# Hybrid decoder layer on one core: ScalarE evacuates the early up-projections, VectorE adds the carried columns

## The chip, the cores and the metric

The kernel runs on one core of one Trainium2 chip. The metric is the device time of one execution in microseconds (us). Engines are named as in the profile: PE is TensorE (PEld its weight loads), DVE is VectorE, ACT is ScalarE, POOL is GpSimd, SP is SyncE, whose queue issues all DMA transfers here.

## The reference

One layer of a hybrid decoder on 1024 tokens of width 1024, in float32. A mixer (RWKV-7 heads beside a causal convolution of width 31) is followed by a gated feed-forward network whose hidden channels pass a causal depthwise convolution of width 3. Cut to what matters here:

```python
D_MODEL, SEQ, D_FF, FFN_CONV_WIDTH = 1024, 1024, 2816, 3

def _conv_ffn(h, ffn_up, ffn_conv_w, ffn_conv_b, ffn_down):
    hid = h @ ffn_up.astype(h.dtype)                       # (1, 1024, 5632)
    hid = _causal_dwconv(hid, ffn_conv_w, ffn_conv_b)      # y[t] = w2 x[t] + w1 x[t-1] + w0 x[t-2] + b
    gate, up = hid[..., :D_FF], hid[..., D_FF:]
    return (jax.nn.gelu(gate, approximate=True) * up) @ ffn_down.astype(h.dtype)

def reference(x, ...):
    h = _rms_norm(x, norm_pre_mix[i])
    mix, v_first = _hybrid_mixer(h, ...)
    x = x + _rms_norm(mix, norm_post_mix[i])
    h = _rms_norm(x, norm_pre_ffn[i])
    x = x + _rms_norm(_conv_ffn(h, ...), norm_post_ffn[i])
    return x
```

## The kernel before

The 1024 tokens are two halves of 512 (HALF); h is 0 for the first, 1 for the second. Activations stand with channels on the 128 partitions and tokens along the free axis. Each float32 factor of a product is split into a high part (a ScalarE copy in the matmul's format) and a low part (the difference, taken by POOL or DVE: the helper `split`, line 174), and a product is three matmuls per block: high x high, high x low, low x high. All matmuls go through the helper at line 147. One up-projection of 128 channels over 512 tokens (`project`) is 24 matmuls into one PSUM bank of 128x512.

The program is written as streams with priorities; a scheduler orders the instructions of each engine ahead of time, by priority and by its own estimate of when things are ready. On the chip each engine runs its list in that order, and waits are semaphores. `high_priority()` moves the instructions traced inside it ahead.

`taps` (lines 914 to 930) does the width-3 convolution on one bank `ps`, for one of the 2 x 22 channel blocks (br 0 is the gate, br 1 the up branch). ScalarE writes `acc = w2*ps + b` (line 921). For h = 0 it also keeps the last two columns in `carry` (line 923). For h = 1 the first two columns of `acc` get the terms of the two tokens before the half, kept in `carry`: three ScalarE instructions on one column each (line 927). Then VectorE adds the other two taps, one instruction each, reading `ps` (line 930); only after the second is the bank free.

Who calls `taps`:

- In the mixer, with h = 0 and banks of the tag pb (two of them): while the RWKV recurrence, the convolution of width 31 (`conv`, whose 30 VectorE taps are line 439) and the output projection are under way, the first-half up-projections of blocks 0 to 6 (EARLY) are run as filler at the lowest priority. Blocks 0, 1 and 6 are whole pairs (`ffn_pair`, two calls of `taps` each). Blocks 2 to 5 are woven with one further gate block each (`ffn_two`, three calls): the first half of a gate's sum goes into a bank and is copied out (line 960), then a projection in another bank, then the second half of the gate. The temporaries are `pt` tiles and `row` tiles.
- In the feed-forward part, with six banks used in turn (pe, pb, xs): `gates` (h = 0), seven whole pairs with h = 1 (`ffn_pair`), and 15 blocks in `shared`. `shared` forms four of the projections' halves from five products and adds of banks (a scheme with fewer products): DVE adds banks at line 1070, among them `W = act1 + y`, after which PE goes on accumulating into y's bank. Each `shared` calls `taps` once with h = 0 and twice with h = 1.

In the shared stage POOL works on the low halves of the weights (line 174) and on sums of weight blocks (line 1113).

Of the kernel before, what the change touches and what calls it, by code (L numbers as in the profile page):

```python
# [16 lines left out]
AF = mybir.ActivationFunctionType  # L17
ALU = mybir.AluOpType
# [4 lines left out]
P = 128  # L23
# [3 lines left out]
HALF = 512  # L27
# [20 lines left out]


BUFS = {"v": 2, "gd": 1, "pt": 6, "kk": 1, "l8": 5, "ca": 6, "ck": 6, "r": 2,  # L50
        "mixr": 1, "co": 4, "po": 1, "c": 4, "t2": 2}

EARLY = 7

# [52 lines left out]
class Trunk:  # L107
    def __init__(self, ctx, tc, a):
        self.ctx, self.tc, self.nc, self.a = ctx, tc, tc.nc, a
        self.at = dict(PRIO)  # L110
        self.n = 0

        self.low_pool = True
        self.low_turn = None

        once = [None]
        self.start = None
        self.homes = {"wr": cycle(once), "wh": cycle(once), "wl": cycle(once)}
# [795 lines left out]
    def taps(self, h, i, br, ps, acc):  # L914

        nc = self.nc
        ch = br * FT + i
        carry = (self.ecarry if i < EARLY + AHEAD else self.fcarry)[:, br, i]
        w = lambda j: self.par("fw", j * 2 * FT + ch)
        with self.tc.high_priority():  # L920
            nc.scalar.activation(acc, ps, AF.Identity, scale=w(2), bias=self.par("fb", ch))
            if h == 0:
                nc.scalar.copy(carry, ps[:, HALF - 2:])
            else:
                for c, k, j in ((0, 1, 1), (0, 0, 0), (1, 1, 0)):
                    a = acc[:, c:c + 1]
                    nc.scalar.activation(a, carry[:, k:k + 1], AF.Identity, scale=w(j), bias=a)
            for j in (1, 0):
                o = 2 - j
                nc.vector.scalar_tensor_tensor(acc[:, o:], ps[:, :HALF - o], w(j), acc[:, o:], ALU.mult, ALU.add)  # L930
# [327 lines left out]
    def run(self):  # L1258
        nc = self.nc
        self.setup()  # L1260
        sts = [{}, {}]
        with ExitStack() as ctx:
            self.setup_mixer(ctx)
            h0 = self.mixer(sts)
        with ExitStack() as ctx:
            self.setup_ffn(ctx)
            h1 = []
            norm = self.norm_ffn(1, lambda: self.row("nrow", 4),
                                 lambda: self.f2p.tile([P, HALF], F32, tag="f2", name=self.nm("m")), h1, 4,
                                 ("pn", "pn2"), pool=self.h1p)  # L1270
            sums = self.parts
            temp = lambda: self.f2p.tile([P, HALF], F32, tag="f2", name=self.nm("acc"))
            act = lambda: self.ap.tile([P, HALF], F32, tag="act", name=self.nm("act"))
            both = [[act() for _ in range(JOINT)] for _ in range(2)]
            turn = cycle((True, False))
            self.gates(h0, both[0][AHEAD:], both[1][AHEAD:],
                       lambda: self.beside(*[norm] if len(h1) == 0 else [norm, sums] if next(turn) else []))
            list(norm)
            S = [[] for _ in range(5)]
            ss = self.act_sums(h0, h1, S)  # L1280
            self.low_turn = cycle((True, True, False))
            for i in range(PLAIN):
                nc.sync.dma_start(self.plain[i], self.ffn_pair(1, h1, i, temp))
                self.beside(*[sums] * (i < PLAIN - 2), *[ss] * (3, 2, 2, 2, 2, 1, 0, 0)[i])
            list(ss)
            list(sums)
            self.low_turn = None
            raws = [self.h1p.tile([P, HALF], F32, tag="h", name=self.nm("b")) for _ in range(8)]
            for m, n in enumerate([*range(AHEAD, JOINT), *range(AHEAD)]):
                self.shared(PLAIN + n, S, h1[4:], both[0][n], both[1][n], raws[m % 2 * 4:m % 2 * 4 + 4] if m else None)  # L1290
                if m < AHEAD:
                    with self.tc.issue_after(self.load.ins):
                        nc.sync.dma_start(both[1][m], self.ahead[m, :, :HALF])
                        nc.sync.dma_start(both[0][m], self.ahead[m, :, HALF:])
            two = self.row("row", 4)
            nc.sync.dma_start(two.rearrange("p (i t) -> p i t", i=2), self.early[:2].rearrange("i p t -> p i t"))
            back = lambda: self.hp.tile([P, HALF], F32, tag="h", name=self.nm("act"))
            second = [back() for _ in range(PLAIN)]
            first = [two[:, :HALF], two[:, HALF:]] + [back() for _ in range(EARLY - 2)]
            for i in range(2, EARLY):  # L1300
                nc.sync.dma_start(first[i], self.early[i])
            for i in range(PLAIN):
                nc.sync.dma_start(second[i], self.plain[i])
            acts = [both[h][AHEAD:] + both[h][:AHEAD] + (first, second)[h] for h in range(2)]
            self.ffn_down(acts)
# [235 lines left out]
```

## Time and profile before

| | |
|---|---|
| median of 3 runs (lowest to highest) | 1257.41 us (1254.89 to 1257.41) |
| the profiled execution | 1255.37 us, span 1253.6 us |
| mean granted PE clock of its core | 0.991 |
| PE busy | 1199.4 us, 96% of the span |
| DVE busy | 919.7 us, 73% |
| ACT busy | 733.3 us, 58% |
| POOL busy | 487.2 us, 39% |
| line 921 (ACT), 18 calls in the mixer | 0.77 to 0.80 us each |
| line 930 (DVE), 36 in the mixer | 26.8 us between 500 and 645 us |
| line 927 (ACT), in the feed-forward part | 132 instructions, median 0.38 to 0.39 us |

In a row of the busy times the share is of the whole span, over stages with different limits. In a row of a group of instructions stand line, engine, operation, the tile written and the tiles read, shapes and count. "[1.49 <-DVE pt L930]" behind an instruction is the idle time of its engine just before it, and the work that ended that idle time.

### The profile page before, as it was taken

To read this page: it belongs to the slowest core of one execution; us is meant where nothing else is said; L and a number is where in the kernel's file an instruction comes from. 1 tells how busy PE (TensorE), PEld (TensorE's weight loads), DVE (VectorE), ACT (ScalarE), POOL (GpSimd) and SP (SyncE) were. 2 spreads that over 40 slices of the span, in tenths; PEclk is the share of its full clock that TensorE was granted. 3 is DMA by queue.
4 is the path that set the end of the run, shared out by engine and by line. 5 is a ranking of instruction groups with operands and counts; after the bars stand their busy time and mean duration, and the time that the engine had idled before them with its cause. 6 is when DMAs were issued, how large, how long until landed. Compare 5 with 4: busy or idle time off the path is not lost.

```text
span 1253.6 us, 22924 instructions
## 1 busy us (share of the span) xinstructions
PE 1199.4 (96%) x8400; PEld 979.7 (78%) x8400; DVE 919.7 (73%) x1591; ACT 733.3 (58%) x1519; POOL 487.2 (39%) x428
## 2 busy tenths in 40 slices
PE   6989999999999988999999999999999999999996
PEld 5767777787778877777888887788888888888885
DVE  5286998898669989988662556777666678479667
ACT  7563564565945676565863587875555566444451
POOL 4343330011103331344445497678888850000002
PEclk9999998999999999999999999999999999999999
DMA  7644442333343362322378898753222334345413
GB/s 244 177 132 138 127 135 71 93 126 124 113 131 90 104 193 85 88 91 85 126 245 297 297 325 267 261 193 93 85 76 76 104 102 164 93 148 190 138 46 135
DMA packets 102960, 182.01 MB, mean 145 GB/s; under 512 B 14944, under 2 KB 21472, under 8 KB 102848
## 3 DMA queue, kind: packets, MB, share of 16 engines
q1 hardware_dynamic: 102848, 180.56, 45.3%
q8 instruction: 66, 1.08, 0.4%
q14 instruction: 46, 0.38, 0.1%
HBM read 138.44 MB, written 42.07 MB: 144 GB/s over the span
## 4 chain that ended last, share of the span: by engine, by line
PE 54%; DVE 10%; DMA 3%; ACT 2%; issue 2%; POOL 1%; SPq 0%; POOLq 0%; DVEq 0%; ACTq 0%
PE pb L147 22%; PE xs L147 14%; PE pe L147 13%; DVE pc L439 3%; PE Y L147 2%; PE pc L147 2%; DMA wr<-w_out 1%; DVE pt L930 1%; POOL wl L174 1%; DMA pt<-mixd 1%; PE pc L162 1%; DVE sub L614 1%; DVE dw L616 0%; DMA po<-post_mix 0%; DVE x L1157 0%
## 5 line engine op out<-in xcount | busy, mean ns | idle before, releaser
L174 POOL TENSOR_TENSOR wl<-wr,wh 128x512 fp32r<-128x512 f32 (+1 forms) x156 | 206.3, 1325 | 229.9 <-ACT wh L174 191.2
L147 PE MATMUL pb<-h,wh 128*128 128x512 f32 (+3 forms) x720 | 228.7, 397 | 3.2 <-ACT wh L174 1.6
L147 PE MATMUL pb<-f,wh 128*128 128x512 f32 x624 | 196.4, 394 | 5.2 <-DVE pt L930 3.6
L174 ACT CAST wh<-wr 128x512 fp32r<-128x512 f32 (+1 forms) x204 | 125.5, 616 | 109.2 <-PE pb L147 34.0
L439 DVE SCALAR_TENSOR_TENSOR pc<-c,params,pc 128x512 f32<-128x512 f32 x232 | 174.4, 752 | 7.3 <-ACT pc L436 3.3
L147 PEld LDWEIGHTS pb<-h,wh 128*128 128x128 f32 (+2 forms) x720 | 131.2, 188 | 35.9 <-ACT wh L174 3.7
L147 PE MATMUL pb<-h,wl 128*128 128x512 f32 (+3 forms) x360 | 146.0, 405 | 2.1 <-POOL wl L174 2.0
L147 PEld LDWEIGHTS pb<-f,wh 128*128 128x128 f32 x624 | 115.5, 188 | 30.1 <-DVE pt L930 4.0
L147 PE MATMUL pb<-f,wl 128*128 128x512 f32 x312 | 122.9, 394 | 0.9 <-POOL wl L174 0.9
L169 POOL TENSOR_TENSOR ss<-var,mhalf 128x1 f32<-128x1 f32 x16 | 11.4, 718 | 223.4 <-DVE var L168 222.7
L174 POOL TENSOR_TENSOR wl<-b,wh 128x512 fp32r<-128x512 f32 x56 | 77.2, 1378 | 21.5 <-ACT wh L174 21.3
L147 PEld LDWEIGHTS pb<-h,wl 128*128 128x128 f32 (+2 forms) x360 | 67.2, 187 | 20.3 <-POOL wl L174 4.3
L1113 POOL TENSOR_TENSOR b<-b,b 128x512 f32<-128x512 f32 x60 | 78.8, 1315 | 3.9 <-DMA wr<-ffn_up 1.8
L174 ACT CAST wh<-b 128x512 fp32r<-128x512 f32 x56 | 34.7, 619 | 68.2 <-PE pb L147 23.3
L147 PEld LDWEIGHTS pb<-f,wl 128*128 128x128 f32 x312 | 58.6, 188 | 14.7 <-POOL wl L174 2.6
L147 PE MATMUL pe<-f,wh 128*128 128x512 f32 x224 | 69.2, 390 | 0.0
L147 PE MATMUL xs<-f,wh 128*128 128x512 f32 x200 | 62.1, 391 | 2.0 <-ACT xs L813 1.3
L174 ACT CAST a<-act 128x512 fp32r<-128x512 f32 x62 | 37.2, 621 | 39.8 <-PE Y L147 18.9
L174 DVE TENSOR_TENSOR a<-act,a 128x512 fp32r<-128x512 f32 x62 | 42.6, 705 | 19.9 <-ACT a L174 19.3
L729 POOL TENSOR_TENSOR XG<-r,GE 64x256 f32<-64x256 f32 x30 | 20.5, 684 | 86.6 <-DVE r L748 81.9
L199 ACT CAST wh<-wr 128x512 fp32r<-128x512 f32 (+2 forms) x44 | 26.6, 606 | 43.4 <-PE pb L147 31.1
L174 ACT CAST w<-wr 128x512 fp32r<-128x512 f32 x38 | 23.6, 623 | 43.2 <-PE Y L147 21.2
(440 smaller groups left out, 2993.6 us busy)
## 6 DMA issues: line engine op xcount, KB each, us to landing
wr<-ffn_up SPq DMA_DIRECT2D x87, 256.0 KB, 3.0
wr<-w_in SPq DMA_DIRECT2D x80, 256.0 KB, 2.9
b<-ffn_up SPq DMA_DIRECT2D x56, 256.0 KB, 2.6
wr<-sums SPq DMA_DIRECT2D x44, 256.0 KB, 2.7
lows<-wl SPq DMA_DIRECT2D x40, 256.0 KB, 3.3
wl<-lows SPq DMA_DIRECT2D x40, 256.0 KB, 2.7
wr<-ffn_down SPq DMA_DIRECT2D x33, 256.0 KB, 2.7
wr<-w_out SPq DMA_DIRECT2D x32, 256.0 KB, 3.3
```

The lines of the kernel that those rows point to most:

```text
L147: return self.nc.tensor.matmul(out, lhsT, rhs, start=start, stop=stop, skip_group_check=skip)
L162: self.nc.tensor.transpose(out, in_, self.con("ident")[:n, :n])
L169: self.nc.gpsimd.tensor_tensor(out, v[:, :n], self.mhalf[:, :n], ALU.pow)
L174: return self.nc.scalar.copy(hi, src), eng.tensor_tensor(lo, src, hi.bitcast(F32), ALU.subtract)
L199: self.nc.scalar.copy(hi, raw)
L439: nc.vector.scalar_tensor_tensor(out, c[:, j:j + HALF], w(j), acc, ALU.mult, ALU.add)
L614: nc.vector.tensor_tensor(tv, dv[:, j + 1:, j:j + 1].broadcast_to([P, n, j]), dv[:, j:j + 1, :j].broadcast_to([P, n, j]), ALU.mult)
L729: nc.gpsimd.tensor_tensor(x[64:128], R[64:128, gs], w.GE[64:128, c, gs].unsqueeze(2).broadcast_to([64, 4, CH]), ALU.mult)
L930: nc.vector.scalar_tensor_tensor(acc[:, o:], ps[:, :HALF - o], w(j), acc[:, o:], ALU.mult, ALU.add)
L1113: sub = lambda o, x, y, op=ALU.subtract: self.nc.gpsimd.tensor_tensor(o, x, y, op)
```

## The change

A flag `mixing` is true while the mixer is traced. While it is, `taps` has ScalarE copy the whole bank to an SBUF tile of a new tag `ev` (two buffers of 128x512), after its first instruction; the carry copy and VectorE's two taps then read that tile, not the bank. In all calls with h = 1, the three one-column ScalarE instructions are replaced by two of VectorE: one on two columns (`acc[:, :2] += carry[:, 0:2] * w0`) and one on one column (`acc[:, :1] += carry[:, 1:2] * w1`). No call with h = 1 is in the mixer.

```diff
 BUFS = {"v": 2, "gd": 1, "pt": 6, "kk": 1, "l8": 5, "ca": 6, "ck": 6, "r": 2,
-        "mixr": 1, "co": 4, "po": 1, "c": 4, "t2": 2}
+        "mixr": 1, "co": 4, "po": 1, "c": 4, "t2": 2, "ev": 2}
...
         self.low_turn = None
+        self.mixing = True
...
         with self.tc.high_priority():
             nc.scalar.activation(acc, ps, AF.Identity, scale=w(2), bias=self.par("fb", ch))
+            if self.mixing:
+                piece = self.tl("ev", [P, HALF])
+                nc.scalar.copy(piece, ps)
+                ps = piece
             if h == 0:
                 nc.scalar.copy(carry, ps[:, HALF - 2:])
             else:
-                for c, k, j in ((0, 1, 1), (0, 0, 0), (1, 1, 0)):
-                    a = acc[:, c:c + 1]
-                    nc.scalar.activation(a, carry[:, k:k + 1], AF.Identity, scale=w(j), bias=a)
+                for n, k, j in ((2, 0, 0), (1, 1, 1)):
+                    a = acc[:, :n]
+                    nc.vector.scalar_tensor_tensor(a, carry[:, k:k + n], w(j), a, ALU.mult, ALU.add)
             for j in (1, 0):
                 o = 2 - j
                 nc.vector.scalar_tensor_tensor(acc[:, o:], ps[:, :HALF - o], w(j), acc[:, o:], ALU.mult, ALU.add)
...
             h0 = self.mixer(sts)
+        self.mixing = False
```

## The prediction

> **What bounds the kernel now.** I read the engines' shares on the page first, then the busy time of each engine by stage, then what TensorE (PE) waited for in the two stages that the change touches.
>
> ```profile
> PE 1199.4 (96%) x8400; PEld 979.7 (78%) x8400; DVE 919.7 (73%) x1591; ACT 733.3 (58%) x1519; POOL 487.2 (39%) x428
> ...
> 500.00:645.00 145.00, 138.73 (x1296) 112.48 (x1295) 114.45 (x180) 92.41 (x187) 60.89 (x50) 1.00 0.35 110
> 760.00:840.00 80.00, 77.73 (x339) 63.01 (x338) 60.72 (x93) 62.45 (x132) 55.57 (x44) 1.00 0.76 249
> 840.00:1030.00 190.00, 190.00 (x839) 157.31 (x839) 125.53 (x186) 109.23 (x228) 159.37 (x122) 1.00 0.30 84
> ```
>
> The columns of the stage rows are length, then busy us of PE, PEld, DVE, ACT and POOL. PE is the bound throughout. 500 to 645 us is the end of the mixer with the early up-projections; 760 to 840 is the whole pairs of the second half; 840 to 1030 is the shared pairs. PE has 6.3 us of holes in the first, 2.3 in the second, none in the third. So a gain can only come out of the 8.6 us of holes, while a loss has no such limit: in the shared stage POOL is busy 84% and DVE 66%, and any new wait of PE there is paid in full. The granted clock is 1.00 in all three.
>
> Next, the waits of PE in the mixer's end (total us, times, longest):
>
> ```profile
> PE pb L147 <- DVE pt L930: 3.6, 3, 1.5
> PE pb L147 <- POOL wl L174: 0.9, 3, 0.4
> ```
>
> The first row is what the change aims at: three times PE stands still because a bank of the tag pb is freed only when VectorE's second tap has read it. One of the three, by engine:
>
> ```profile
> 525.79 0.78 ACT L921 ACTIVATE pt<-pb,params 128x512 f32<-128x512 f32 x1
> 526.47 0.15 ACT L923 COPY ecarry<-pb 128x2 f32<-128x2 f32 x1
> ...
> 528.39 0.74 DVE L930 SCALAR_TENSOR_TENSOR pt<-pb,params,pt 128x511 f32<-128x511 f32 x1
> 529.05 0.75 DVE L439 SCALAR_TENSOR_TENSOR pc<-c,params,pc 128x512 f32<-128x512 f32 x1
> 529.71 0.75 DVE L930 SCALAR_TENSOR_TENSOR pt<-pb,params,pt 128x510 f32<-128x510 f32 x1
> ...
> 530.50 0.72 PE L147 MATMUL pb<-f,wh 128*128 128x512 f32 x2 [1.49 <-DVE pt L930]
> ```
>
> ScalarE has read the bank by 526.6; VectorE, with convolution taps (L439) between its own, frees it at 530.46 and PE resumes at 530.50.
>
> **The change, part by part: the mixer's taps.** The mixer holds 18 calls of taps: three whole pairs with two, four woven ones with three. Each gets a ScalarE copy of the bank to an SBUF piece. The same copy exists in this stage already:
>
> ```profile
> L960 ACT COPY row<-pb x4: 580/584/595, 528.9 to 606.1; 128x512 f32<-128x512 f32 x4
> ```
>
> 18 x 0.584 = 10.5 us more on ACT, which is busy 92.4 of 145 us; its 52.6 idle us cover it on average. In the example the bank comes free at about 526.57 + 0.58 = 527.2 instead of 530.46, before PE wants it, and the same shift of some 3 us exceeds all three waits (longest 1.5). So I take 3.6 us as gone; the next thing late is POOL's low half of a weight, already 0.9 us in three waits. Queued on ACT behind the new copy are the weight casts and the recurrence's copies, 0.58 us later where they follow directly; between projections of 24 matmuls ACT has room for that, and I put 0.2 us on it. The taps begin about 0.4 us later (they wait for the 0.58 copy, no longer for the 0.15 one), which only the gate product and its store follow. The carry copy now reads the piece and holds no bank. Two pieces last two projections, over 10 us, so the bank does not wait for a piece.
>
> What speaks against it is what the taps now read. A DVE instruction with a PSUM operand keeps its length while POOL runs; with two SBUF inputs it does not:
>
> ```profile
> L439 DVE SCALAR_TENSOR_TENSOR pc<-c,params,pc x232: 723/756/757, 134.2 to 582.0; 128x512 f32<-128x512 f32 x116
> ...
> L897 DVE SCALAR_TENSOR_TENSOR nrow<-m,nr,nrow x8: 739/751/1726, 704.8 to 719.6; 128x512 f32<-128x512 f32 x8
> ...
> L616 DVE TENSOR_TENSOR dw<-dw,sub x56: 174/203/1329, 117.5 to 504.6; 128x14 f32<-128x14 f32 x8, 128x26 f32<-128x26 f32 x8, 128x36 f32<-128x36 f32 x8, 128x44 f32<-128x44 f32 x8
> ...
> 500.58 1.30 POOL L174 TENSOR_TENSOR wl<-wr,wh 128x512 fp32r<-128x512 f32 x1 [7.97 <-ACT wh L174]
> 500.74 1.21 DVE L616 TENSOR_TENSOR dw<-dw,sub 128x50 f32<-128x50 f32 x1
> ```
>
> Minimum, median and maximum in ns: L439 (one SBUF input, sum in PSUM) never exceeds 757 in 232; L897 (both inputs SBUF) reaches 1726; L616, some 0.2 us alone, reaches 1329. The last two rows show why: the small instruction issued at 500.74 ends with POOL's, at 501.9. The Trainium skill, page "SBUF — State Buffer", section "Who interferes with whom", says that a VectorE instruction with two SBUF inputs contends with a GpSimd instruction that reads SBUF, and that whichever starts second is blocked fully. The rows agree; by that rule the 36 mixer taps, free of it now, become subject to it, and so do the new carried columns below.
>
> Price in the mixer: POOL is busy 42% of the stage with pieces of 1.3 us, so 36 taps x 0.42 x 0.65 = 9.8 us more on DVE (114.5 of 145 now, 124 then). DVE does not feed PE directly there; the last convolution tap starts at 582.0 and the output projection begins after 636, which covers it. POOL in its turn is held up by up to a tap's 0.75 us and hands weights over late. Between 0 (always slack) and 3.6 us (all that was won) I take the present 0.9 us of such waits doubled, as those rows are the only ones that show tight handovers: +0.9. Mixer in all: -3.6 + 0.2 + 0.9 = -2.5 us.
>
> **The carried columns, second half.** 44 calls (7 whole pairs and 15 shared ones, two each) lose three ScalarE instructions and gain two of VectorE.
>
> ```profile
> 760.00:840.00 80.00, 14.15 (x42) 1.00 0.76 249
> 840.00:1030.00 190.00, 28.02 (x84) 1.00 0.30 84
> ...
> L369 DVE SCALAR_TENSOR_TENSOR row<-carry,params,row x8: 210/219/220, 205.5 to 279.5; 128x1 f32<-128x1 f32 x8
> ```
>
> ACT loses 28.0 us between 840 and 1030 (84 instructions of line 927) and 14.2 between 760 and 840. This alone is worth nothing: PE has no hole in the shared stage, and ACT is not what it waits for. DVE gains 88 instructions; the nearest row, a one-column addition of just this kind, takes 0.22 us, and chained about 0.2 each. Both inputs are in SBUF, so POOL's 84% is what matters. One shared pair in the steady pattern (period 13.6 us):
>
> ```profile
> 899.19 0.70 DVE L1070 TENSOR_TENSOR pb<-act,pb 128x512 f32<-128x512 f32 x1 [0.16 <-PE pb L147]
> 899.80 0.74 DVE L930 SCALAR_TENSOR_TENSOR acc<-pe,params,acc 128x511 f32<-128x511 f32 x1
> ...
> 902.97 1.53 DVE L930 SCALAR_TENSOR_TENSOR act<-pb,params,act 128x511 f32<-128x511 f32 x2
> 904.41 0.68 DVE L1070 TENSOR_TENSOR acc<-act,xs 128x512 f32<-128x512 f32 x1
> ...
> 897.91 1.29 POOL L174 TENSOR_TENSOR wl<-b,wh 128x512 fp32r<-128x512 f32 x1
> 899.16 1.30 POOL L1113 TENSOR_TENSOR b<-b,b 128x512 f32<-128x512 f32 x1
> 900.41 1.30 POOL L174 TENSOR_TENSOR wl<-wr,wh 128x512 fp32r<-128x512 f32 x1
> 902.00 1.60 POOL L174 TENSOR_TENSOR wl<-b,wh 128x512 fp32r<-128x512 f32 x1 [0.29 <-ACT wh L174]
> 904.70 1.30 POOL L174 TENSOR_TENSOR wl<-b,wh 128x512 fp32r<-128x512 f32 x1 [1.09 <-ACT wh L174]
> ...
> 906.70 0.62 PE L147 MATMUL xs<-f,wh 128*128 128x512 f32 x2
> ```
>
> DVE is in one unbroken burst from 899.19, and near its end stands the sum W (904.41 to 905.09), which reads bank xs; PE goes on adding into that bank at 906.70. The slack is 1.6 us, and the next period repeats it. Into this burst go four small instructions. Bare, 4 x 0.2 = 0.8 us: hidden. With POOL, whose row is closed from 897.91 to 901.71: the first, around 898.95, waits for the end at 899.20 (0.25); the second meets the next piece half way on average (0.7); the later two, after 902, find POOL's gaps of 0.3 and 1.1 us, so one half wait of 0.35. Burst: 0.8 + 0.25 + 0.7 + 0.35 = 2.1, over the slack by 0.5; x 14 periods = +7 us. Ends: 0, if the waits stay under 0.8 in all; and, if each of the four is hit at POOL's 84% for half a piece, 0.8 + 4 x 0.84 x 0.65 - 1.6 = 1.4, x 14 = 19 us. I take the value between, as POOL's rows have gaps in one half of the burst and none in the other.
>
> In the whole pairs, 28 such instructions on DVE (60.7 of 80 us) cost 28 x 0.2 = 5.6 us and, at POOL's 69%, up to 28 x 0.69 x 0.65 = 12.6 of waiting: DVE would nearly fill. Against that its own idle time there goes:
>
> ```profile
>   ACT acc L927: 8.6, 5
> ```
>
> (8.6 us in which taps waited for the three ScalarE instructions.) PE's reliance on DVE there is loose (six banks in turn), so between -1 and +6 I take +2.
>
> **Sum:** 1255.4 (the profiled execution, whose span is 1253.6) - 2.5 + 7 + 2 = 1261.9. That execution lies 2.0 us under the median of the runs, 1257.4, and 0.5 over the lowest; I leave the sum where it comes out.
>
> **Rivals.** (1) Faster: the small instructions fit the slack. Its point is total POOL waits under 0.8 us a period; it would be so if DVE's fixed order put W before the taps of the third bank, or the columns into POOL's gaps. Then only the mixer counts: 1255.4 - 3.6 to - 1 = 1251.8 to 1254.4. For it: 0.22 us is little, DVE has a third of the stage free. Against: the burst is unbroken, and POOL closed over its first half. (2) No change: the mixer's 2.5 us are eaten by 0.1 us a period and the whole pairs; 1254.9 to 1257.9. (3) Slower in the mixer itself: ACT copies and late low halves cost PE more than 3.6 us, while the second half is calm; 1258 to 1261. Against it: PE's holes behind POOL are 0.9 us now. That the banks are not freed earlier is excluded by the in-order rows above: nothing but the copy holds them.
>
> **Chances.** Forecast (stalls in the shared stage, 1258 to 1275) 0.50; (1) 0.30; (2) 0.15; (3) 0.05. About 0.2%, 2.5 us, is what a measurement tells from no change here. Faster 0.30, same 0.15, slower 0.55. Range 1251.5 to 1275; the forecast's own, 1258 to 1275.
>
> **What the profile after would show.** Right: the row of PE waiting for DVE pt gone; 18 new ScalarE copies of 0.58; mixer taps with maxima well over 0.757; carried columns of 0.2 to 1.5 us; and, deciding, PE with new waits for DVE in the shared stage, whose period rises from 13.6 to about 14.1. Wrong: that period unchanged, since then rival (1) holds; or the mixer's end longer by more than the 2.5 us it should lose. DVE's order around W is what I know least.

## The result and the profile after

The changed kernel takes 1269.01 us (median of 6 runs, 1266.31 to 1271.33) against 1257.41 us (6 runs, 1254.89 to 1259.5) of the kernel before: ratio 1.0092 [1.0073, 1.0112], 11.6 us slower. The profiled execution after took 1271.33 us, with a span of 1269.5: it is the slowest of its runs, while the one before was among its fastest, so the two traces differ by more than the medians, 15.9 us of span.

The page's row of busy times after:

```profile
PE 1206.8 (95%) x8400; PEld 980.3 (77%) x8400; DVE 979.8 (77%) x1679; ACT 701.2 (55%) x1403; POOL 484.3 (38%) x428
```

The same three stages as before, by windows (length, then busy us of PE, PEld, DVE, ACT and POOL, PE's granted clock, DMA share, GB/s):

```profile
500.00:645.00 145.00, 139.46 (x1273) 111.39 (x1271) 120.08 (x184) 99.76 (x200) 59.90 (x48) 0.99 0.32 99
760.00:840.00 80.00, 77.24 (x331) 62.48 (x330) 72.07 (x117) 51.05 (x89) 52.95 (x41) 0.98 0.74 240
840.00:1030.00 190.00, 182.18 (x792) 147.52 (x791) 150.55 (x222) 76.56 (x132) 153.02 (x121) 1.00 0.29 84
```

The shared stage (last row), which had PE busy for 190.00 of 190 us, now has 7.8 us of holes, at the same clock, and 47 matmuls fewer begin in it. DVE's busy time there rises by 25 us, ACT's falls by 33, as the instructions moved (and fewer blocks fit into the window). What PE waits for between 840 and 1060 us (total us, times, longest; before, this view had no row):

```profile
PE pb L148 <- DVE acc L1075: 3.9, 6, 0.9
PE xs L148 <- DVE acc L1075: 2.2, 4, 0.5
PE xs L148 <- ACT pb L1112: 1.8, 1, 1.8
```

Line numbers have moved: L1075 is the former 1070, and its `acc` is the sum W; L1112 is the gelu. The carried columns are L932 (minimum/median/maximum in ns):

```profile
L932 DVE SCALAR_TENSOR_TENSOR acc<-ecarry,params,acc x36: 205/512/1339, 763.7 to 1054.3; 128x2 f32<-128x2 f32 x18, 128x1 f32<-128x1 f32 x18
L932 DVE SCALAR_TENSOR_TENSOR acc<-fcarry,params,acc x22: 471/666/916, 848.8 to 995.2; 128x2 f32<-128x2 f32 x11, 128x1 f32<-128x1 f32 x11
L932 DVE SCALAR_TENSOR_TENSOR act<-fcarry,params,act x22: 207/683/1317, 854.0 to 1000.6; 128x2 f32<-128x2 f32 x11, 128x1 f32<-128x1 f32 x11
```

Their busy time in the shared stage, by windows:

```profile
840.00:1030.00 190.00, 34.66 (x51) 1.00 0.29 84
```

An instruction on one or two columns takes 0.2 us undisturbed and 0.68 us on average (34.66 / 51). One burst, from DVE's timeline:

```profile
921.68 0.56 DVE L932 SCALAR_TENSOR_TENSOR acc<-fcarry,params,acc 128x2 f32<-128x2 f32 x1 [1.57 <-ACT fcarry L928]
922.16 0.74 DVE L935 SCALAR_TENSOR_TENSOR acc<-xs,params,acc 128x511 f32<-128x511 f32 x1
922.82 0.67 DVE L932 SCALAR_TENSOR_TENSOR acc<-fcarry,params,acc 128x1 f32<-128x1 f32 x1
...
927.91 1.49 DVE L932 SCALAR_TENSOR_TENSOR act<-fcarry,params,act 128x2 f32<-128x2 f32 x2
929.32 0.74 DVE L935 SCALAR_TENSOR_TENSOR act<-pe,params,act 128x511 f32<-128x511 f32 x1
929.98 0.67 DVE L1075 TENSOR_TENSOR acc<-act,pb 128x512 f32<-128x512 f32 x1
```

POOL's timeline beside it:

```profile
920.93 1.29 POOL L1118 TENSOR_TENSOR b<-wr,b 128x512 f32<-128x512 f32 x1
922.18 1.29 POOL L175 TENSOR_TENSOR wl<-b,wh 128x512 fp32r<-128x512 f32 x1
...
928.09 1.29 POOL L175 TENSOR_TENSOR wl<-b,wh 128x512 fp32r<-128x512 f32 x1 [0.66 <-ACT wh L175]
```

And PE's:

```profile
929.87 0.39 PE L148 MATMUL pb<-f,wl 128*128 128x512 f32 x1
930.79 0.70 PE L148 MATMUL pb<-f,wh 128*128 128x512 f32 x2 [0.54 <-DVE acc L1075]
```

Add start and length: the three entries of L932 end at 922.24, 923.49 and 929.40, and the POOL instructions beside them at 922.22, 923.47 and 929.38. The entry at 927.91 is two instructions: the first began ahead of POOL's and took 0.21 us, the second was held. So three of the four are released when POOL's big one is done. The taps between them (one SBUF input, the other in PSUM) keep their 0.74 us. W ends at 930.65, and PE, which adds into W's bank next, resumes at 930.79. Its row says 0.54 us of idle time; from start to start it is more, 0.92 us where the same step takes 0.22 elsewhere in the stage, and the pair after it takes 0.55 where 0.46 is usual: 0.8 us lost in this period.

In the mixer, PE's four longest waits between 495 and 705 us:

```profile
PE pe L163 <- DVE mixr L770: 2.1, 1, 2.1
PE pb L148 <- ACT wm L175: 1.4, 1, 1.4
PE pb L148 <- ACT ev L925: 1.3, 2, 0.9
PE pe L148 <- ACT pe L814: 0.7, 1, 0.7
```

ScalarE's new copies (L925), and the taps that read them:

```profile
L925 ACT COPY ev<-pb x18: 567/576/597, 504.8 to 645.9; 128x512 f32<-128x512 f32 x18
L935 DVE SCALAR_TENSOR_TENSOR pt<-ev,params,pt x28: 737/751/1843, 510.2 to 647.7; 128x511 f32<-128x511 f32 x14, 128x510 f32<-128x510 f32 x14
```

The wait for taps (3.6 us before) is gone. In its place stand one for the recurrence (mixr), one for a weight's cast and two for the new copy.

Where the time went, worked out from the traces' matmul records: how much later than in the trace of before the matmul stands that began there at the given time (us).

| kernel | 497 (mixer's filler begins) | 704 | 761 | 840 | 1020 |
|---|---|---|---|---|---|
| after | 1.1 | 2.9 | 2.8 | 4.9 | 16.1 |
| columns only (e1) | 0.7 | 2.6 | 2.6 | 2.2 | 14.7 |
| copies only (e2) | 1.4 | 3.4 | 3.3 | 3.3 | 3.3 |
| columns, kept ones in PSUM (e3) | 0.3 | -0.3 | -0.3 | -0.6 | -0.6 |
| columns, GpSimd lightened (e7) | 0.2 | 0.3 | 0.3 | -0.3 | -0.3 |
| whole change, kept columns in PSUM (e8) | 0.4 | 4.2 | 4.1 | 4.3 | 5.9 |

In after, 11.2 of 16 us arise in the shared stage, and nothing after it. They are eleven stalls of PE. Ten are waits for W: eight cost 0.8 us each, one 1.2 and one 1.05. The first, at 859 us, costs 2.1; there PE waits for a gelu, and the gelu for taps behind four held columns (4.0 us for the four). What lies ahead of 497 us is unchanged code.

### The profile page after: what moved, and what is told of

It reads as the page before. It is cut to its first block, busy times and chain, and to the rows that moved or that the text cites. A ratio compares the mean times of both kernels' runs of the same rounds, so it can differ in the third digit from the quotient of the medians.

```text
span 1269.5 us, 22863 instructions
## 1 busy us (share of the span) xinstructions
PE 1206.8 (95%) x8400; PEld 980.3 (77%) x8400; DVE 979.8 (77%) x1679; ACT 701.2 (55%) x1403; POOL 484.3 (38%) x428
## 4 chain that ended last, share of the span: by engine, by line
PE 42%; DVE 20%; ACT 5%; issue 2%; DMA 2%; POOL 1%; SPq 0%; POOLq 0%; DVEq 0%; ACTq 0%
PE pb L148 18%; PE xs L148 10%; PE pe L148 9%; DVE pc L440 3%; DVE acc L935 3%; PE Y L148 2%; DVE acc L932 2%; PE pc L148 2%; ACT acc L922 1%; DVE act L932 1%; DVE act L1110 1%; DMA wr<-ffn_up 1%; DMA wr<-w_out 1%; DVE act L935 1%; PE pc L163 1%
## 5 line engine op out<-in xcount | busy, mean ns | idle before, releaser
L175 POOL TENSOR_TENSOR wl<-b,wh 128x512 fp32r<-128x512 f32 x56 | 73.0, 1304 | 30.3 <-ACT wh L175 30.3
L148 PEld LDWEIGHTS pb<-f,wl 128*128 128x128 f32 x312 | 59.2, 190 | 14.1 <-POOL wl L175 1.6
L175 ACT CAST wh<-b 128x512 fp32r<-128x512 f32 x56 | 34.5, 615 | 38.3 <-issue 11.2
```

Of the source, the lines that this page charges most:

```text
L148: return self.nc.tensor.matmul(out, lhsT, rhs, start=start, stop=stop, skip_group_check=skip)
L175: return self.nc.scalar.copy(hi, src), eng.tensor_tensor(lo, src, hi.bitcast(F32), ALU.subtract)
```

## Experiments

Theory A: the loss is the carried columns' collision with GpSimd in the shared stage. Rival B: it is the longer or reordered VectorE list itself, GpSimd or no. Rival C: it is the mixer's copies. Ratios are against the kernel before on the same chip; each "only" is an edit of before.

**e1: the columns alone.**

```diff
-                for c, k, j in ((0, 1, 1), (0, 0, 0), (1, 1, 0)):
-                    ... nc.scalar.activation(a, carry[:, k:k + 1], AF.Identity, scale=w(j), bias=a)
+                for n, k, j in ((2, 0, 0), (1, 1, 1)):
+                    ... nc.vector.scalar_tensor_tensor(a, carry[:, k:k + n], w(j), a, ALU.mult, ALU.add)
```

> The kernel before with the carried columns on VectorE in all 44 calls, and no copies in the mixer. If the two edits add up, the loss of 4.9 to 16.1 us along TensorE's progress in the changed kernel (its second half) is all the columns': +13 us (+11 shared stage, +2 whole pairs), so about 1268 to 1270, with the mixer's end as before. Rival, that the mixer's copies shift what the second half meets (memory, order, transfers): clearly less than +10.

1269.76 us, ratio 1.0096 [1.0066, 1.0126]: the whole loss. PE's three longest waits between 760 and 1035 us:

```profile
PE pb L147 <- DVE acc L1070: 4.3, 6, 1.2
PE xs L147 <- DVE acc L1070: 2.7, 5, 0.6
PE xs L147 <- ACT pb L1107: 1.8, 1, 1.8
```

The same waits for W as after. C falls as the main cause; A and B both remain.

**e2: the copies alone.**

```diff
             nc.scalar.activation(acc, ps, AF.Identity, scale=w(2), bias=self.par("fb", ch))
+            if self.mixing:
+                piece = self.tl("ev", [P, HALF])
+                nc.scalar.copy(piece, ps)
+                ps = piece
```

> The 18 copies in the mixer alone, carried columns on ScalarE as before. My prediction's step says -2.5 us (1253 on the profiled execution's footing). The trace of the changed kernel says +1.6 at the end of the mixer against its beginning, so +1 to +2. Whichever comes out, TensorE should have no wait on VectorE's pt taps left; if the sum stays positive, the 3.6 us must be seen in new waits on other work (the recurrence's chain, weights).

1260.03 us, 1.0009 [0.9994, 1.0024]: no measurable change, and no gain. PE's longest waits between 495 and 705 us:

```profile
PE pe L163 <- DVE mixr L770: 2.1, 1, 2.1
PE pb L148 <- ACT wm L175: 1.4, 1, 1.4
PE pb L148 <- ACT ev L925: 1.2, 2, 0.9
```

These are the waits of after: they belong to the copies. The 36 taps' busy time between 497 and 705 us, first of before:

```profile
497.00:705.00 208.00, 26.78 (x36) 1.00 0.48 155
```

and of e2:

```profile
497.00:705.00 208.00, 35.90 (x36) 0.99 0.47 150
```

9.1 us more on DVE.

**e3: the columns alone, with one input moved to PSUM.** In the shared stage ScalarE copies the two kept columns into an idle bank, and VectorE's two instructions read them there. They are as many, in a similar order, with one SBUF input instead of two.

```diff
+            if h == 1 and self.sharing:
+                held = self.bank(("pn", "pn2")[br])[:, :2]
+                nc.scalar.copy(held, carry)
+                carry = held
```

> As columns only, but in the 15 shared blocks ScalarE first copies the two kept columns (128x2) into a PSUM bank that is idle there, and VectorE's two instructions read them from it: the same count of VectorE instructions, one SBUF input instead of two. Theory, POOL's and VectorE's shared reads: each small instruction takes 0.2 us in place of a mean of 0.5 to 0.7, TensorE's waits for the sum W go, the shared stage returns to 190 us per 14 periods, and the kernel lies about 11 us under columns only. Rival, that the mere number of instructions in the unbroken burst does it: no gain, the waits of 0.5 us a period stay.

1258.78 us, 1.0005 [0.9984, 1.0026]: the loss is gone. Rows of the small instructions, two of the shared stage and one of the whole pairs, where they still read SBUF:

```profile
L932 DVE SCALAR_TENSOR_TENSOR acc<-Y,params,acc x30: 207/211/221, 843.4 to 1039.5; 128x2 f32<-128x2 f32 x15, 128x1 f32<-128x1 f32 x15
L932 DVE SCALAR_TENSOR_TENSOR act<-pc,params,act x30: 205/208/221, 848.3 to 1042.3; 128x2 f32<-128x2 f32 x15, 128x1 f32<-128x1 f32 x15
L932 DVE SCALAR_TENSOR_TENSOR acc<-ecarry,params,acc x28: 208/657/1342, 760.6 to 833.4; 128x2 f32<-128x2 f32 x14, 128x1 f32<-128x1 f32 x14
```

The shared stage from 845 us on:

```profile
845.00:1035.00 190.00, 190.00 (x840) 157.34 (x839) 142.39 (x244) 88.26 (x174) 150.53 (x117) 1.00 0.32 93
```

Sixty instructions, none over 221 ns, beside a POOL that is as busy as ever (150.5 us); the 28 with two SBUF inputs, in the same run, go up to 1342. The Trainium skill, page "SBUF — State Buffer", section "Who interferes with whom", says that a VectorE instruction with at most one SBUF input (outside the two-port modes) does not contend with GpSimd; these rows agree. DVE's list differs from that of e1 in places (W stands behind both taps of its bank here, behind one of them in e1), so B is nearly out, not quite; e7 closes it.

**e7: the columns alone, GpSimd lightened.** In the shared stage three of the four sums of weight blocks are left out, so the output is not that of the layer.

```diff
-        sub(b12, b12, b11)
-        sub(b11, t3, b11, ALU.add)
-        sub(b21, b21, b11)
+        if not self.sharing:
+            ...
```

> Columns only, with three of the four block sums of GpSimd (line 1113) left out in the shared stage, so that weights there are not the right ones: GpSimd's busy share of that stage falls from 79% to about 50%, VectorE's instructions and their order stay. If the collision with GpSimd's reads is the cause: the small instructions' mean falls, TensorE's waits for W fall from 7 us to under 2, the kernel lies 8 to 11 us under columns only. If the length of VectorE's own burst is the cause: waits for W stay near 7 us.

1256.69 us, 0.9991 [0.9974, 1.0008], some 13 us under e1. The columns are L928 here. Their rows in the shared stage:

```profile
L928 DVE SCALAR_TENSOR_TENSOR acc<-fcarry,params,acc x22: 207/216/222, 843.6 to 980.4; 128x2 f32<-128x2 f32 x11, 128x1 f32<-128x1 f32 x11
L928 DVE SCALAR_TENSOR_TENSOR act<-fcarry,params,act x22: 208/216/219, 849.0 to 985.3; 128x2 f32<-128x2 f32 x11, 128x1 f32<-128x1 f32 x11
```

The stage:

```profile
840.00:1030.00 190.00, 190.00 (x840) 157.34 (x839) 139.05 (x242) 83.63 (x144) 105.18 (x82) 1.00 0.30 84
```

The burst of DVE that answers to the one above:

```profile
897.98 0.22 DVE L928 SCALAR_TENSOR_TENSOR acc<-fcarry,params,acc 128x2 f32<-128x2 f32 x1 [1.57 <-ACT fcarry L924]
898.78 0.21 DVE L928 SCALAR_TENSOR_TENSOR acc<-fcarry,params,acc 128x1 f32<-128x1 f32 x1
903.44 0.46 DVE L928 SCALAR_TENSOR_TENSOR act<-fcarry,params,act 128x2 f32<-128x2 f32 x2
904.48 0.68 DVE L1071 TENSOR_TENSOR acc<-act,xs 128x512 f32<-128x512 f32 x1
```

POOL beside it:

```profile
896.24 1.30 POOL L175 TENSOR_TENSOR wl<-b,wh 128x512 fp32r<-128x512 f32 x1 [1.41 <-ACT wh L175]
899.42 1.30 POOL L175 TENSOR_TENSOR wl<-wr,wh 128x512 fp32r<-128x512 f32 x1 [1.89 <-ACT wh L175]
901.68 1.29 POOL L175 TENSOR_TENSOR wl<-b,wh 128x512 fp32r<-128x512 f32 x1 [0.96 <-ACT wh L175]
904.40 1.30 POOL L175 TENSOR_TENSOR wl<-b,wh 128x512 fp32r<-128x512 f32 x1 [1.43 <-ACT wh L175]
```

And PE's next use of W's bank:

```profile
906.40 0.62 PE L148 MATMUL xs<-f,wh 128*128 128x512 f32 x2
```

In its steady periods DVE runs the same list as in after, but the small instructions now come in POOL's gaps (897.54 to 899.42, 902.97 to 904.40). From the first of them to W's end it takes 905.16 - 897.98 = 7.18 us; in after, 930.65 - 921.68 = 8.97. Before, the burst began with a tap, and W ended at 905.09, 6.81 us later:

```profile
898.28 0.75 DVE L930 SCALAR_TENSOR_TENSOR acc<-pb,params,acc 128x511 f32<-128x511 f32 x1 [1.57 <-ACT fcarry L923]
```

The slack behind W is 906.40 - 905.16 = 1.24 us here. In after the way is 1.79 us longer; against 1.24 of slack that leaves about 0.55, and PE's row in after says 0.54. B falls: the list without the collision fits. Leaving the sums out took work off POOL that could matter elsewhere too; PE was never short of it in the shared stage before, so this is not what brought the 13 us.

**e8: the whole change, kept columns in PSUM in the shared stage** (the edits of e3 on top of after).

> The whole change, copies and columns, but in the 15 shared blocks the kept columns are read from an idle PSUM bank, as in columns with PSUM. If the parts add: the time of copies only, within 0.2% of before (1256 to 1260), so that the whole loss of the change hangs on where 60 instructions of two columns or one read their kept columns.

1259.85 us, 1.0015 [0.9999, 1.0032]. The parts add: the loss of after falls from 11.6 to 1.9 us, which is e2 (+1.1) and e3 (+0.6) together. Its trace keeps one stall in the shared stage, 1.6 us at 858, again for the gelu. What stands in the way there is the gate product, which has two SBUF inputs in every kernel here:

```profile
850.48 3.96 DVE L1115 TENSOR_TENSOR act<-act,acc 128x512 f32<-128x512 f32 x1
```

At the same place it takes 0.68 us in after. In e6 and e10, whose second half is that of before, it takes 2.92 and 3.02 us, and PE loses 0.7 and 0.8. So GpSimd can hold up this stage without the columns too.

**e4 and e6: copies in four of the 18 calls** (up-branch calls only; one kernel, run twice).

```diff
-            self.taps(0, j, br, ps, accs[br])
+            self.taps(0, j, br, ps, accs[br], br == 1 and n < AHEAD - 1)
```

> The kernel before with a ScalarE copy for only four of the mixer's 18 calls: those whose bank the next projection wants while the other bank holds a half-finished gate (three of them are where TensorE waited 3.6 us). Carried columns on ScalarE as before. If the freed bank is what counts: -2 to -4 us, three waits gone with 14 copies fewer than in copies only. If a freed bank is only exchanged for a wait on something else of the mixer (in-order TensorE, the recurrence's chain): within 1.5 us of before.

> The four-copies kernel again with more rounds, for its 0.15%: if the freed bank is worth something, 0.998 with an interval under 1; if the waits only move to other calls (its trace had two waits on taps, 4.8 us), 1.000.

0.9985 [0.9969, 1.0002], then 1.0009 [0.9994, 1.0024]: no change. PE's wait for taps moved to other calls, between 495 and 705 us:

```profile
PE pb L147 <- DVE pt L934: 4.8, 2, 3.0
```

It was 3.6 us in three, longest 1.5; now 4.8 in two.

**e5 and e10: dead copies** (one kernel, run twice). All 18 copies are made, but nothing reads the piece: the taps and, other than the expectation of e5 says, the carry copy read the bank as before.

```diff
+            if self.mixing:
+                piece = self.tl("ev", [P, HALF])
+                nc.scalar.copy(piece, ps)
```

> Copies only, but the 18 copies are read by nobody except the carry copy: VectorE's taps go on reading the bank, which is held until the second tap as before. It prices what the copies cost by themselves (18 x 0.58 us of ScalarE) and in the order of the lists. If the ScalarE copies delay casts that TensorE needs: above before by 1 us or more, waits of TensorE on VectorE's taps still about 3.6 us. If the copies are free and copies only got nothing because the freed banks were exchanged for waits on the recurrence's chain: within 1 us of before.

> Dead copies again with more rounds, beside the one before: if its 0.997 is its own, 0.997 with an interval clear of 1.

1253.90 us, 0.9970 [0.9956, 0.9984], and on another chip 1253.42 us, 0.9971 [0.9955, 0.9987]. Work that serves nothing makes the kernel 3.7 us faster, reproducibly; this version beats both kernels. What is left as a cause is the order (by exclusion, no run isolates it): with the added copies the scheduler lays the engines' lists of the mixer out differently, and PE is idle 6.0 and 7.0 us between the two matmuls that stand at 497 and 704 us in the table above, where it was 8.5.

**e9: first tap from the piece, second from the bank.** The dead copies, with half of the taps colliding and the bank held as before.

```diff
+                src = piece if self.mixing and j == 1 else ps
+                nc.vector.scalar_tensor_tensor(acc[:, o:], src[:, :HALF - o], w(j), acc[:, o:], ALU.mult, ALU.add)
```

> Dead copies, with one difference: VectorE's first tap reads the SBUF piece, the second still the bank, which is held as long. TensorE's list differs from that of dead copies in small local swaps alone. So 18 of VectorE's instructions get a second SBUF input, nothing is freed. If the collision with GpSimd's reads is what eats the gain in the mixer: 18 x 0.25 us (9.1 us more over 36 taps in copies only) = 4.5 us more on VectorE, and 1 to 3 us more than dead copies. If it is covered there and only the order of the lists counts: within 1 us of dead copies.

1264.65 us, 1.0062 [1.0038, 1.0086]: +7.8 us, which neither theory had. The taps' busy time between 497 and 705 us:

```profile
497.00:705.00 208.00, 28.19 (x36) 0.99 0.46 148
```

PE's longest waits there:

```profile
PE pb L148 <- DVE pt L935: 4.3, 5, 1.0
PE pc L163 <- DVE co L440: 1.2, 1, 1.2
```

The taps are only 1.4 us longer than before, while PE's idle time rises from 8.5 to 13.7 us. Its longest wait ends just behind that window, at the end of the mixer (495 to 715 us):

```profile
PE xs L148 <- DVE act L1015: 4.2, 1, 4.2
```

It was 0.4 us before. VectorE's copy L1015 waited 4.64 us for the landing of a store (`mixd<-c`). SyncE issued that store at 702.86 us, 1.9 us after its data were there, as it had other stores (`sums<-pt`) to issue first; before, those were issued from 686.85 us on, well ahead. So 3.8 of the 5.2 us come from the order of SyncE's list; the rest is not explained. Of the collision e9 says nothing: inconclusive for what it was made for.

**e11: dead copies of 64 columns.**

> Dead copies of 64 columns in place of 512 (about 0.2 us in place of 0.58). Nothing is freed and ScalarE gets 3 to 4 us instead of 10. If the gain of dead copies is only the order that the scheduler's estimate happens to give, this one, with another order (324 lines of difference on TensorE), lands anywhere within 3 us of before, and its waits of TensorE lie in other places. If the copies as such help (by spacing ScalarE's work), it gains less than dead copies but gains.

1260.56 us, 1.0022 [1.0006, 1.0038]. A shorter dead copy loses 2.8 us where the long one wins 3.7. Both leave the banks, the taps and the second half alone.

## Why the prediction was right, and where it was not

The forecast, "stalls in the shared stage, 1258 to 1275", held: 1269.0 against 1262. Point by point:

- **Shared stage, +7 us: right in mechanism, too small.** PE does wait for W, since two-SBUF-input instructions stand behind POOL's. The burst was to be 0.5 us over its slack; by the rows above it is 0.55. The waiting in the burst was put at 1.3 us and was 1.83 (2.72 us for the four instructions against 0.89 in e7); the bare instructions, put at 0.8, lengthened the way to W by less, 0.37 us (7.18 in e7 against 6.81 from 898.28 to 905.09 before), because the order around them changed: one of the two taps of the third bank now stands behind W. That these two errors cancel is luck. What was mis-sized is what an excess costs PE: 0.8 us from start to start, and not the 0.5 that the row calls idle, as the pair after the stall is slower too (0.55 for 0.46) and the idle time is counted from the modelled end of the matmul before. Nor are the stalls 14 alike: the eleven named above make 10.8 of the 11.2 us. That is inside the term's own ends of 0 and 19.
- **Whole pairs, +2 us: not there.** In e1, e3, e7 and e8, which all have VectorE's columns reading SBUF in that stage, the lateness between 761 and 840 us changes by -0.4, -0.3, -0.6 and +0.2 us. In after it is +2.1, in an execution whose clock was 0.98 in that stage, against 1.00; PE's idle time there is only 0.5 us more than before. The small instructions are as slow as in the shared stage (median 657 ns in e3), but PE's waits only changed hands: 1.1 us for a gelu, 0.7 for POOL and 0.3 for a tap before; 1.3 for a tap and 0.5 to 0.7 for POOL in e1, e3 and e7. The term should have been 0.
- **Mixer, -2.5 us: the step that failed.** Its parts were seen rightly: the wait for taps went from 3.6 us to nothing, the copies take 0.576 us each (0.584 was used), the taps take 9.1 us longer in e2 and 7.2 (33.97 for 26.78) in after (9.8 was used). Failed is "the next thing late is POOL's low half of a weight", with 3.6 us taken as gone. POOL's waits even fell to 0.6 us; others came that the rows of before could not show, for the recurrence (2.1), a cast (1.4) and the copy itself (1.3). PE's idle time between the matmuls that stand at 497 and 704 us above fell by 0.4 to 1.6 us only, where the copies are read:

| kernel | stretch, us | PE idle, us | clock, 497 to 705 us |
|---|---|---|---|
| before | 207.0 | 8.5 | 1.00 |
| mixer unchanged: e1, e3, e7 | 208.9, 206.5, 207.1 | 8.4, 7.9, 8.5 | 0.99, 1.00, 1.00 |
| copies read: after, e2, e8 | 208.8, 209.0, 210.7 | 7.6, 8.1, 6.9 | 0.99, 0.99, 0.98 |
| four copies: e4, e6 | 208.1, 206.8 | 8.5, 8.6 | 0.99, 1.00 |
| dead copies: e5, e10 | 204.4, 203.9 | 6.0, 7.0 | 0.99, 1.00 |
| half of the taps: e9 | 215.7 | 13.7 | 0.99 |
| small dead copies: e11 (its slowest run) | 213.2 | 9.6 | 0.98 |

  Copies that nobody reads move the time by -3.7 us (e5, e10) to +2.8 (e11), with no bank freed and no tap changed. A term of -2.5 is within that, and could not be had from the waits of one order. The stretch itself also varies by 2.4 us between executions whose mixer is the same (206.5 to 208.9), partly with the clock, so one trace can't show a gain or loss of this size.
- **Rival 1** (faster; columns fit the slack) states the right point: the waits of POOL in a burst must stay under 0.8 us. e7 is that case (0.89 us for all four, the bare price, and no loss), but it takes a lighter POOL. Its other condition came half true: W moved ahead of one of the third bank's two taps, and the loss came all the same. **Rival 2** has the time that e8 gives (1.0015), a kernel without the columns' collision in the shared stage. **Rival 3**: the mixer is not where it slows; e2 costs 1.1 us [-0.8, +3.0].
- **Of the signs named**, all that spoke for the forecast came: no row of DVE pt, 18 copies, taps up to 1843 ns, columns of 205 to 1339 ns, PE's waits for DVE; the period, where it had a stall of 0.8, rose from 13.6 to 14.4, not 14.1.
- **In sum:** the runs give about +1 (e2), 0 and +11 to +12.5 us in place of -2.5, +2 and +7. The forecast of the time came as near as it did partly because the pairs' error takes 2 us off the other two.

Left open: what the taps' collision in the mixer costs by itself, as no kernel here had the collision with the order unchanged; what makes the order of e5 better than that of before; and what makes the gate product meet so many of POOL's pieces in some executions.

## What to carry to other kernels

Before a small instruction is moved to VectorE, count its SBUF inputs and look at what GpSimd does then: beside 1.3 us pieces a 0.2 us instruction with two SBUF inputs costs 0.7, and one input in PSUM brings it back to 0.2. Price the excess over a slack by what a stall costs from start to start, not by the idle time of its row. Where a scheduler rebuilds the lists, measure a neutral edit too (here a dead copy): a gain smaller than what such an edit does (here -0.3 to +0.2%) can't be read off the waits that an edit removes.

## What was not expected of the hardware

An instruction on one or two columns is held by POOL to the end of POOL's instruction, as one on 512 is: 1339 ns at most against some 205 undisturbed, and in the burst shown ending within 0.02 us of POOL's end. An instruction can also be held by several pieces: the gate product of e8, from 850.48 to 854.44 us, ends 0.55 us after the last of three that POOL runs without a gap (850.07 to 853.89). And a stall of PE was longer than its row says: 0.54 us of idle time stood for 0.8 us of lost progress in a period.
